# Transposing a as 32-bit pairs of bf16 columns in a two-stage matmul with GELU

## The chip, the cores and the metric

The kernel runs on one core of a Trainium2 chip. The time is device time in microseconds, the median of several runs. The engines are named as the profile names them: PE is TensorE (its weight loads are PEld), DVE is VectorE, ACT is ScalarE, POOL is GpSimd, SP is SyncE, which only issues DMAs here.

## The reference

Inputs are float32: a is 1024 x 1024, b is 1024 x 2048, c is 2048 x 1024.

```python
def reference(a, b, c):
    h = np.matmul(a, b)
    h = 0.5 * h * (1 + np.tanh(np.sqrt(2 / np.pi) * (h + 0.044715 * h ** 3)))
    return np.matmul(h, c).astype(np.float32)
```

## The kernel before

The kernel keeps everything in SBUF as bf16 and writes the program order of every engine by hand (a manual schedule): each engine works its instructions off in the order in which they stand in the code, and waits by semaphores for what the others produce.

TensorE contracts over the partitions, so for h = a b both operands need the contraction index k on the partitions. b has it there as loaded. a does not: it is loaded with its rows on the partitions and must be transposed. The result, aT, has k on the partitions and the rows of a (two halves h = 0, 1 of H = 512) along the free dimension.

The first part of a (halves 0 and 1 of columns 0 to 255, and half 0 of columns 256 to 511) and of b comes by SP's queue as float32 into `sta` and `stb` and is cast to bf16 on VectorE and ScalarE (`cast_a`, `cast_b`). The rest is loaded by POOL's queue with a cast on the way: `abq` for a, `b1` and `b2` for b, `c_sb` for c. These loads stand in one list, and after the eighth each issue waits for the landing of the load eight places ahead of it.

`turn(h, q, i, ab)` is the transposition of 256 columns of a for one half h, in bank i of PSUM. It is a generator: for each n of two blocks of 128 columns it issues four TensorE transposes (128x128 bf16, the piece of a as weights, the identity as the moving operand) and one VectorE copy from PSUM to `aT`; then it yields, and the caller puts matmuls between. Nearly all turns use bank 7.

The stages in order:

1. The first quarter of b's columns, tiles t = 0 to 3 (128 columns each), plainly: `block(h, tiles, ks)` adds the contraction slices ks to the accumulators `ps[h, t]` by `mm1` (one matmul of 128x512, line L114). The eight accumulators (two halves, four tiles) would fill all eight banks, so `ps[1, 3]` is done at the end of the stage and bank 7 serves the turns until then. The k loop follows the arrival of a and b. Turns (0,0), (1,0), (0,1), (1,1), ... stand between the blocks. While the first data is awaited, `stir` issues matmuls on zeros.
2. `seven(zero, ...)`: the second quarter of b's columns, by a scheme of seven products instead of eight (Strassen's, in Winograd's form). Its operands are sums and differences that VectorE makes in float32r: t1 to t4 from the four blocks of aT, s1 to s4 from those of b. Two of the products, P1 and P2, read aT and b directly. The t's are made partly during stage 1 (`zero.t1`, `zero.t2`, `zero.t3`, line L170).
3. `seven(one, ...)`: the other half of b's columns in the same way with the same t's.
4. `seven(two, ...)`: GELU(h) times c, with the seven products again, and the stores.

In stages 2 to 4 the order is P1, P2, P5, P6, P7, and then P4 and P3 (in stage 2) or P3 and P4. All products are issued at line L212. `snap` (L298) copies a PSUM bank to SBUF on ScalarE, `plus` (L303) adds a bank and such a copy on VectorE; the functions `between0` and `between1` place the VectorE work of the operands between the products.

The order around the turns in the loop of stage 1 is, before the change:

```python
    for q in range(1, 3):
        k = 2 * q
        block(0, range(4), (k,))
        tn = turn(1, q, 7, abq[:, q, 1])
        next(tn)
        block(0, range(4), (k + 1,))
        next(tn)
        zero.t1(4, q)
```

Of the kernel before, what the change touches and what calls it, by code (L numbers as in the profile page):

```python
# [9 lines left out]
F32 = mybir.dt.float32  # L10
F32R = mybir.dt.float32r
BF16 = mybir.dt.bfloat16
# [7 lines left out]
def kernel(ctx, tc, a, b, c, out):  # L20
    nc = tc.nc
    M, K = a.shape
    _, N = b.shape
    _, P = c.shape
    H = 512
    KT = K // 128
    NT = N // 128

    av = a.rearrange("(mt p) k -> p mt k", p=128)
    bv = b.rearrange("(kt p) n -> p kt n", p=128)  # L30
    cv = c.rearrange("(nt p) q -> p nt q", p=128)

    ctx.enter_context(tc.manual_schedule())
    consts = ctx.enter_context(tc.tile_pool(name="consts", bufs=1))
# [5 lines left out]
    def slot(tag, shape, dt, name):  # L40
        return big.tile(shape, dt, name=name, tag=tag)

    def bank(i, shape=(128, H), dt=F32, name="ps"):
        return pp.tile(list(shape), dt, name=name, tag=f"bank{i}", padded_shape=None)

    def pieces(tag, bufs, shape, dt, name):
        return small.tile(shape, dt, name=name, tag=tag, bufs=bufs)

    warm = nc.const_aps.tensor(0.0, [128, 256], F32)
    ident = consts.tile([128, 128], BF16, name="ident")  # L50
    make_identity(nc, ident)
    gate = consts.tile([128, 1], F32, name="gate")
    g = consts.tile([128, 1], F32, name="g")

    consts.tile([128, 16], F32, name="room")

    c_sb = keep.tile([128, NT, P], BF16, name="c_sb")
    hT = [keep.tile([128, NT, H], BF16, name=f"hT{h}") for h in range(2)]
    aT = slot("a", [128, 2, KT, H], BF16, "aT")
    b1 = slot("b1", [128, KT, 1024], BF16, "b1")  # L60
    b2 = slot("b2", [128, KT, 1024], BF16, "b2")

# [2 lines left out]
    stb = slot("x0", [128, KT, H], F32, "stb")  # L65
    sta = slot("x1", [128, 2, 2, 4, 256], F32, "sta")
    abq = slot("x3", [128, 4, 2, 4, 256], BF16, "abq")

    def a_part(h, q):
        return av[:, 4 * h:4 * h + 4, ds(q * 256, 256)]  # L70

    def b_part(q):
        return bv[:, 2 * q:2 * q + 2, 0:H]

    nc.sync.dma_start(out=sta[:, 0, 0], in_=a_part(0, 0))  # L75
    nc.sync.dma_start(out=stb[:, 0:2], in_=b_part(0))  # L76
    nc.sync.dma_start(out=sta[:, 1, 0], in_=a_part(1, 0))
    nc.sync.dma_start(out=sta[:, 0, 1], in_=a_part(0, 1))
    nc.sync.dma_start(out=stb[:, 2], in_=bv[:, 2, 0:H])

    nc.gpsimd.tensor_copy(gate, sta[:, 0, 0, 3, 0:1])
    nc.scalar.activation(g, warm[:, 0:1], AF.Gelu_apprx_tanh)
# [2 lines left out]
    def cast_load_a(h, q):  # L85
        nc.gpsimd.dma_start(out=abq[:, q, h], in_=a_part(h, q))

    def cast_load_b(q):
        nc.gpsimd.dma_start(out=b1[:, 2 * q:2 * q + 2, 0:H], in_=b_part(q))

    cast_load_a(1, 1)
    nc.gpsimd.dma_start(out=b1[:, 3, 0:H], in_=bv[:, 3, 0:H])
    for q in range(2, 4):
        cast_load_a(0, q)
        cast_load_b(q)
        cast_load_a(1, q)
    for k in range(0, KT, 4):
        nc.gpsimd.dma_start(out=b1[:, k:k + 4, H:], in_=bv[:, k:k + 4, ds(H, H)])
    for n in range(2):
        for k in range(0, KT, 4):  # L100
            nc.gpsimd.dma_start(out=b2[:, k:k + 4, ts(n, H)],
                                in_=bv[:, k:k + 4, ds(1024 + n * H, H)])
    for t in range(0, NT, 2):
        nc.gpsimd.dma_start(out=c_sb[:, t:t + 2], in_=cv[:, t:t + 2])  # L104

    def copy(eng, dst, src):
        if eng is nc.scalar:
            nc.scalar.activation(dst, src, AF.Copy)
        else:
            nc.vector.tensor_copy(dst, src)  # L110

    def mm1(p, t, h, ks):
        for k in ks:
            nc.tensor.matmul(p, b1[:, k, ts(t, 128)], aT[:, h, k],  # L114
                             start=(k == 0), stop=(k == KT - 1))

    def gelu(t, h, p):
# [2 lines left out]
    ps = {(0, t): bank(t) for t in range(4)}  # L120

    def stir(*widths):

        for w in widths:
            nc.tensor.matmul(ps[0, 3][:, 0:w], warm[:, 0:128], warm[:, 0:w],
                             start=True, stop=True, skip_group_check=True)

    def cast_a(h, q, *engs):

        ab = pieces("ab", 2, [128, 4, 256], BF16, "ab")  # L130
        for i, eng in enumerate(engs):
            w = 256 // len(engs)
            for j, e in enumerate(eng if isinstance(eng, tuple) else (eng,)):
                m = slice(2 * j, 2 * j + 2) if isinstance(eng, tuple) else slice(0, 4)
                copy(e, ab[:, m, ts(i, w)], sta[:, h, q][:, m, ts(i, w)])
        return ab

    def turn(h, q, i, ab):

        banks = i if isinstance(i, tuple) else (i,)  # L140
        pts = [bank(x, (128, 2, H), BF16, "pt") for x in banks]
        for n in range(2):
            pt = pts[n % len(pts)]
            for m in range(4):
                nc.tensor.transpose(pt[:, n, ts(m, 128)], ab[:, m, ts(n, 128)], ident)  # L145
            nc.vector.tensor_copy(aT[:, h, 2 * q + n], pt[:, n])  # L146
            yield

    def cast_b(k, *engs):
        c0 = 0  # L150
        for i, eng in enumerate(engs):
            w = (H - c0) if i == len(engs) - 1 else H // len(engs) // 128 * 128
            copy(eng, b1[:, k, ds(c0, w)], stb[:, k, ds(c0, w)])
            c0 += w

    def block(h, tiles, ks):
        for k in ks:
            for t in tiles:
                mm1(ps[h, t], t, h, (k,))


    class Seven:
        def __init__(self, kt, A, B, s, t, n=4):
            self.kt, self.A, self.B, self.s, self.t, self.n = kt, A, B, s, t, n
# [51 lines left out]
    def pair(i):  # L216
        x = slot(f"x{i}", [128, 2, 4, H], F32R, "x1")
        return x[:, 0], x[:, 1]

    BB = [[aT[:, 0, 0:4], aT[:, 1, 0:4]], [aT[:, 0, 4:8], aT[:, 1, 4:8]]]  # L220

    def quarters(b, c0, w):
        return [[b[:, 0:4, ds(c0, w)], b[:, 4:8, ds(c0, w)]],
                [b[:, 0:4, ds(c0 + w, w)], b[:, 4:8, ds(c0 + w, w)]]]

    zero = Seven(4, quarters(b1, H, 256), BB, [None] * 4, [None] * 4, 2)
    one = Seven(4, quarters(b2, 0, H), BB, [None] * 4, zero.t)

    stir(256, 256, 256, 256, 256)
    tn = turn(0, 0, 4, cast_a(0, 0, nc.vector))  # L230
    next(tn)
    stir(128)
    cast_b(0, nc.vector, nc.vector, nc.scalar)
    next(tn)
    stir(64)
    cast_b(1, nc.scalar)
    ab = cast_a(1, 0, nc.vector, nc.scalar)
    block(0, range(4), (0,))
    block(0, range(2), (1,))
    for _ in turn(1, 0, (7, 6), ab):  # L240
        pass
    block(0, range(2, 4), (1,))
    ab = cast_a(0, 1, (nc.scalar, nc.vector), nc.vector)
    cast_b(2, nc.scalar, nc.scalar)
    for t in range(3):
        ps[1, t] = bank(4 + t)
    zero.t[0], zero.t[1] = pair(2)
    block(1, range(3), (0,))
    tn = turn(0, 1, 7, ab)
    next(tn)  # L250
    block(1, range(3), (1,))
    next(tn)
    zero.t1(4, 0)
    for q in range(1, 3):
        k = 2 * q
        block(0, range(4), (k,))
        tn = turn(1, q, 7, abq[:, q, 1])
        next(tn)
        block(0, range(4), (k + 1,))
        next(tn)  # L260
        zero.t1(4, q)
        block(1, range(3), (k,))
        tn = turn(0, q + 1, 7, abq[:, q + 1, 0])
        next(tn)
        block(1, range(3), (k + 1,))
        next(tn)
    zero.t1(4, 3)
    block(0, range(4), (6, 7))
    zero.t2(2, 0)
    for t in range(4):  # L270
        gelu(t, 0, ps[0, t])
    ps[1, 3] = bank(7)
    mm1(ps[1, 3], 3, 1, range(2))
    tn = turn(1, 3, 0, abq[:, 3, 1])
    next(tn)
    mm1(ps[1, 3], 3, 1, range(2, 5))
    next(tn)
    mm1(ps[1, 3], 3, 1, (5,))
    zero.t[2], x11 = pair(1)
    zero.t[3], x31 = pair(3)  # L280
    zero.plain_t(2, 0)
    zero.t3(2, 0)
    zero.t2(2, 1)
    block(1, range(3), (6, 7))
    mm1(ps[1, 3], 3, 1, range(6, 8))
    for t in range(4):
# [99 lines left out]
    def between0(n):  # L386
        if n == "P1":
            zero.plain_s()
            zero.plain_t(2, 1)
        elif n == "P2":  # L390
            zero.t3(2, 1)
            zero.s3()
            zero.t4(t4, 2)
            one.last_t = t4
            zero.s4(x31[:, :, 256:])
# [19 lines left out]
    zero.s1()  # L415
    zero.s2()
    seven(zero, done0, between0)
    one.s[3] = slot("b1", [128, 2, 4, H], F32R, "x1")[:, 0]
    one.s1()
# [68 lines left out]
```

## Time and profile before

| what | value |
|---|---|
| median of 3 runs | 117.55 us (117.53 to 117.62) |
| span of the profiled execution | 115.7 us |
| its own time beside the span | not recorded apart from the span; the median is 1.85 us above it |
| PE busy | 111.1 us (96%), 542 matmuls and as many weight loads |
| DVE / ACT / POOL busy | 90.0 (78%) / 51.4 (44%) / 17.2 (15%) us |
| granted clock of TensorE | 1.000 |
| DMA | 15.94 MB moved, 138 GB/s mean |

How to read it. The span runs from the first to the last instruction of the profiled execution. In lists of instructions each line has the start and the duration in microseconds, the engine, the line of the code, the operation, out<-in by the program's names, the shapes, how many, and in brackets how long the engine had been idle and what ended that. In groups by line the numbers behind the bar are the busy time in microseconds and the mean duration of one in nanoseconds, and behind the next bar the idle time just before them. Matmuls are pipelined: one lasts some 380 ns in the records while a new one starts every 216 ns, so times on TensorE are taken from start to start.

### The profile page before, as it was taken

How to read it: one execution, taken by the hardware profiler on the slowest of the kernel's cores; microseconds unless marked ns; L12 is line 12 of the kernel's file. 1: busy time of each engine (PE TensorE's matmuls, PEld its weight loads, DVE VectorE, ACT ScalarE, POOL GpSimd, SP SyncE). 2: the span in 40 equal slices, each digit the busy share in tenths (PEclk: the TensorE clock that was granted, in tenths of full speed). 3: DMA queues.
4: the chain of work that ended last, by engine and by line, in shares of the span. 5: the costliest groups of instructions: out<-in, count | busy, mean ns of one | idle time of the engine just before them, and what ended most of it. 6: DMA issues, size and time to landing. Idle time of an engine off the chain costs nothing.

```text
span 115.7 us, 1461 instructions
## 1 busy us (share of the span) xinstructions
PE 111.1 (96%) x542; PEld 77.1 (67%) x542; DVE 90.0 (78%) x107; ACT 51.4 (44%) x86; POOL 17.2 (15%) x29
## 2 busy tenths in 40 slices
PE   7989999999999999999999999999999999999980
PEld 6645555546776447888885444688888888888860
DVE  0347748789999998935699999999999986954770
ACT  5053000999259997166698429500124982000000
POOL 2497755223322000000000000000000000000000
PEclk9999999999999999999999999999999999999999
DMA  2999999999999999998000000060000002014993
GB/s 69 295 381 229 200 199 205 204 208 205 206 211 209 212 213 209 212 210 168 8 0 0 6 0 0 38 235 0 0 0 0 0 4 91 1 73 176 370 363 106
DMA packets 13414, 15.94 MB, mean 138 GB/s; under 512 B 736, under 2 KB 9312, under 8 KB 13408
## 3 DMA queue, kind: packets, MB, share of 16 engines
q0 software_dynamic: 8672, 9.31, 47.6%
q1 hardware_dynamic: 4736, 6.56, 15.8%
q8 instruction: 4, 0.07, 0.3%
q14 instruction: 2, 0.02, 0.0%
HBM read 20.97 MB, written 4.19 MB: 218 GB/s over the span
## 4 chain that ended last, share of the span: by engine, by line
PE 90%; DMA 5%; SPq 1%; DVE 1%; issue 0%
PE ps L212 76%; PE ps L114 11%; DMA sta<-in_a_dram 5%; PE pt L145 3%; SPq L76 0%; DVE ab L110 0%; SPq L75 0%; DVE ot L375 0%
## 5 line engine op out<-in xcount | busy, mean ns | idle before, releaser
L212 PE MATMUL ps<-x,s 128*128 128x512 f32 x128 | 29.6, 391 | 0.0
L212 PEld LDWEIGHTS ps<-x,s 128*128 128x128 f32 x128 | 24.0, 188 | 5.1
L212 PE MATMUL ps<-x,x 128*128 128x512 f32 x96 | 22.9, 394 | 0.0
L212 PEld LDWEIGHTS ps<-x,x 128*128 128x128 f32 x96 | 18.0, 188 | 3.9
L114 PE MATMUL ps<-aT,b 128*128 128x512 bf16 x64 | 16.1, 379 | 0.2 <-DVE b L110 0.2
L298 ACT ACTIVATE v<-ps 128x512 f32<-128x512 f32 x10 | 6.0, 599 | 19.1 <-PE ps L212 19.1
L212 PE MATMUL ps<-c_sb,hT 128*128 128x512 bf16 (+1 forms) x72 | 14.2, 356 | 0.0
L212 PE MATMUL ps<-x 128*128 128x512 f32 x56 | 13.2, 392 | 0.0
L212 PEld LDWEIGHTS ps<-x 128*128 128x128 f32 x56 | 10.2, 188 | 2.6 <-ACT u L298 0.4
L118 ACT ACTIVATE hT<-ps 128x512 bf16<-128x512 f32 x14 | 7.3, 595 | 9.7 <-PE ps L114 9.7
L212 PEld LDWEIGHTS <-hT 128*128 128x128 bf16 x72 | 6.9, 98 | 7.0 <-issue 0.5
L118 ACT ACTIVATE hT<-ot 128x512 bf16<-128x512 f32 x18 | 10.4, 624 | 2.0 <-DVE ot L303 2.0
L212 PE MATMUL ps<-aT,b 128*128 128x512 bf16 x48 | 10.7, 379 | 0.0
L146 DVE COPY aT<-pt 128x512 bf16<-128x512 bf16 x16 | 6.7, 423 | 5.1 <-PE pt L145 5.1
L303 DVE TENSOR_TENSOR ot<-ps,u 128x512 f32<-128x512 f32 x10 | 6.7, 690 | 5.1 <-ACT u L298 5.1
L303 DVE TENSOR_TENSOR ot<-ps,v 128x512 f32<-128x512 f32 x10 | 6.7, 688 | 4.8 <-DMA out_dram<-ot 3.8
L170 DVE TENSOR_TENSOR x<-c_sb 128x1024 fp32r<-128x1024 bf16 x8 | 9.3, 1226 | 0.0
L114 PEld LDWEIGHTS <-b 128*128 128x128 bf16 x64 | 5.7, 98 | 4.5 <-DVE b L110 0.3
L212 PEld LDWEIGHTS <-b 128*128 128x128 bf16 x48 | 4.6, 98 | 5.7 <-issue 0.3
L104 POOL DMA_DIRECT2D c_sb<-in_c_dram x8 | 5.6, 702 | 13.1 <-DMA b<-in_b_dram 12.4
L170 DVE TENSOR_TENSOR x<-b 128x1024 fp32r<-128x1024 bf16 (+1 forms) x4 | 7.0, 1752 | 0.6 <-issue 0.6
L298 ACT ACTIVATE u<-ps 128x512 f32<-128x512 f32 x10 | 5.9, 598 | 3.4 <-PE ps L212 3.2
(44 smaller groups left out, 111.3 us busy)
## 6 DMA issues: line engine op xcount, KB each, us to landing
c_sb<-in_c_dram POOLq DMA_DIRECT2D x8, 512.0 KB, 20.0
out_dram<-ot SPq DMA_DIRECT2D x13, 256.0 KB, 2.1
b<-in_b_dram POOLq DMA_DIRECT2D x6, 512.0 KB, 15.3
sta<-in_a_dram SPq DMA_DIRECT2D x3, 512.0 KB, 6.1
abq<-in_a_dram POOLq DMA_DIRECT2D x5, 256.0 KB, 7.9
out_dram<-ot SPq DMA_DIRECT2D x6, 128.0 KB, 2.0
stb<-in_b_dram SPq DMA_DIRECT2D x1, 512.0 KB, 5.3
b<-in_b_dram POOLq DMA_DIRECT2D x2, 256.0 KB, 8.2
```

Of the source, the lines that this page charges most:

```text
L104: nc.gpsimd.dma_start(out=c_sb[:, t:t + 2], in_=cv[:, t:t + 2])
L114: nc.tensor.matmul(p, b1[:, k, ts(t, 128)], aT[:, h, k], start=(k == 0), stop=(k == KT - 1))
L118: nc.scalar.activation(hT[h][:, t], p, AF.Gelu_apprx_tanh)
L145: nc.tensor.transpose(pt[:, n, ts(m, 128)], ab[:, m, ts(n, 128)], ident)
L146: nc.vector.tensor_copy(aT[:, h, 2 * q + n], pt[:, n])
L170: nc.vector.tensor_tensor(out=dst[:, r], in0=x[:, r], in1=y[:, r], op=op)
L212: nc.tensor.matmul(p[:, ds(c0, w)], l[:, k, ts(j, 128)], r[:, k, ds(c0, w)], start=(start and k == 0), stop=(k == self.kt - 1), skip_group ...
L298: nc.scalar.activation(st, p, AF.Copy)
L303: nc.vector.tensor_tensor(out=ot, in0=p, in1=st, op=ADD)
```

## The change

A bf16 piece of a is taken as 32-bit words, each of two neighbouring columns, and transposed as float32: four transposes of 128x128 words do what eight bf16 ones did. What comes out has on partition p the columns 2p and 2p + 1 of the 256, side by side. The layout of `aT` becomes [128, 2, KT / 2, H, 2], the pair being the last index; one VectorE copy of 512 float32 words per turn takes the place of two of 512 bf16. A contraction slice is therefore no longer 128 neighbouring rows of b, but the even or the odd rows of 256; b is loaded accordingly (`bq`), and the matmuls read every second bf16 of `aT`. The class `Turned` gives stages 2 and 3 the same view of aT.

The turns are now put between single matmuls: `block` takes a generator and issues one transpose ahead of each of its matmuls. The casts of a are split by rows and no longer by columns. The b loads of POOL's queue behind the first are 12 of 256 KB (written) in place of 6 of 512 KB. `zero.t1(4, q)` stands at the end of the loop; `zero.t1(4, 3)`, both halves of `zero.t2` and the first half of `zero.t3` move later.

```diff
-    bv = b.rearrange("(kt p) n -> p kt n", p=128)
+    bq = b.rearrange("(q p r) n -> p q r n", p=128, r=2)
...
-    ident = consts.tile([128, 128], BF16, name="ident")
+    ident = consts.tile([128, 128], F32, name="ident")
...
-    aT = slot("a", [128, 2, KT, H], BF16, "aT")
+    aT = slot("a", [128, 2, KT // 2, H, 2], BF16, "aT")
...
-        return bv[:, 2 * q:2 * q + 2, 0:H]
+        return bq[:, q, :, 0:H]
+
+    def b_load(tile_, q, n0):
+        nc.gpsimd.dma_start(out=tile_[:, 2 * q:2 * q + 2, ds(n0 % 1024, H)], in_=bq[:, q, :, ds(n0, H)])
...
-    for k in range(0, KT, 4):
-        nc.gpsimd.dma_start(out=b1[:, k:k + 4, H:], in_=bv[:, k:k + 4, ds(H, H)])
-    for n in range(2):
-        for k in range(0, KT, 4):
-            nc.gpsimd.dma_start(out=b2[:, k:k + 4, ts(n, H)],
-                                in_=bv[:, k:k + 4, ds(1024 + n * H, H)])
+    for n0, tile_ in ((H, b1), (1024, b2), (1024 + H, b2)):
+        for q in range(4):
+            b_load(tile_, q, n0)
...
-            nc.tensor.matmul(p, b1[:, k, ts(t, 128)], aT[:, h, k],
+            nc.tensor.matmul(p, b1[:, k, ts(t, 128)], aT[:, h, k // 2, :, k % 2],
...
-        banks = i if isinstance(i, tuple) else (i,)
-        pts = [bank(x, (128, 2, H), BF16, "pt") for x in banks]
-        for n in range(2):
-            pt = pts[n % len(pts)]
-            for m in range(4):
-                nc.tensor.transpose(pt[:, n, ts(m, 128)], ab[:, m, ts(n, 128)], ident)
-            nc.vector.tensor_copy(aT[:, h, 2 * q + n], pt[:, n])
+        pt = bank(i, (128, H), F32, "pt")
+        for m in range(4):
+            nc.tensor.transpose(pt[:, ts(m, 128)], ab[:, m].bitcast(F32), ident)
+            if m == 3:
+                nc.vector.tensor_copy(aT[:, h, q].rearrange("p m r -> p (m r)").bitcast(F32), pt)
             yield
...
-    def block(h, tiles, ks):
+    def block(h, tiles, ks, turns=()):
+        turns = iter(turns)
         for k in ks:
             for t in tiles:
+                next(turns, None)
                 mm1(ps[h, t], t, h, (k,))
+        for _ in turns:
+            pass
...
+    class Turned:
+        def __init__(self, h, k0):
+            self.h, self.k0 = h, k0
+
+        def __getitem__(self, at):
+            k = at[1]
+            if isinstance(k, slice):
+                k0, n = self.k0 + k.start, k.stop - k.start
+                q, r = divmod(k0, 2)
+                return aT[:, self.h, q, :, r:r + n].rearrange("p m r -> p r m")
+            q, r = divmod(self.k0 + k, 2)
+            return aT[:, self.h, q, at[2] if len(at) > 2 else slice(0, H), r]
...
     stir(256, 256, 256, 256, 256)
-    tn = turn(0, 0, 4, cast_a(0, 0, nc.vector))
-    next(tn)
-    stir(128)
+    ab = cast_a(0, 0, nc.vector)
+    for n, _ in enumerate(turn(0, 0, 4, ab)):
+        if n == 3:
+            stir(256, 128)
     cast_b(0, nc.vector, nc.vector, nc.scalar)
-    next(tn)
-    stir(64)
     cast_b(1, nc.scalar)
-    ab = cast_a(1, 0, nc.vector, nc.scalar)
+    ab = cast_a(1, 0, (nc.scalar, nc.vector))
     block(0, range(4), (0,))
-    block(0, range(2), (1,))
-    for _ in turn(1, 0, (7, 6), ab):
-        pass
-    block(0, range(2, 4), (1,))
-    ab = cast_a(0, 1, (nc.scalar, nc.vector), nc.vector)
+    block(0, range(4), (1,), turn(1, 0, 7, ab))
+    ab = cast_a(0, 1, (nc.scalar, nc.vector))
     cast_b(2, nc.scalar, nc.scalar)
...
-    block(1, range(3), (0,))
-    tn = turn(0, 1, 7, ab)
-    next(tn)
+    block(1, range(3), (0,), turn(0, 1, 7, ab))
     block(1, range(3), (1,))
-    next(tn)
     zero.t1(4, 0)
     for q in range(1, 3):
         k = 2 * q
-        block(0, range(4), (k,))
-        tn = turn(1, q, 7, abq[:, q, 1])
-        next(tn)
+        block(0, range(4), (k,), turn(1, q, 7, abq[:, q, 1]))
         block(0, range(4), (k + 1,))
-        next(tn)
+        block(1, range(3), (k,), turn(0, q + 1, 7, abq[:, q + 1, 0]))
+        block(1, range(3), (k + 1,))
         zero.t1(4, q)
-        block(1, range(3), (k,))
-        tn = turn(0, q + 1, 7, abq[:, q + 1, 0])
-        next(tn)
-        block(1, range(3), (k + 1,))
-        next(tn)
-    zero.t1(4, 3)
     block(0, range(4), (6, 7))
-    zero.t2(2, 0)
...
-    mm1(ps[1, 3], 3, 1, range(2))
     tn = turn(1, 3, 0, abq[:, 3, 1])
-    next(tn)
-    mm1(ps[1, 3], 3, 1, range(2, 5))
-    next(tn)
-    mm1(ps[1, 3], 3, 1, (5,))
+    for k in range(4):
+        mm1(ps[1, 3], 3, 1, (k,))
+        next(tn)
+    mm1(ps[1, 3], 3, 1, (4, 5))
+    zero.t1(4, 3)
+    zero.t2(2)
     zero.t[2], x11 = pair(1)
     zero.t[3], x31 = pair(3)
     zero.plain_t(2, 0)
-    zero.t3(2, 0)
-    zero.t2(2, 1)
...
         elif n == "P2":
-            zero.t3(2, 1)
+            zero.t3(2)
```

More of the change, by code (lines that the diff above doesn't have):

```diff
@@ L53 @@
     g = consts.tile([128, 1], F32, name="g")
-    consts.tile([128, 16], F32, name="room")
+    consts.tile([128, 80], F32, name="room")
     c_sb = keep.tile([128, NT, P], BF16, name="c_sb")
     hT = [keep.tile([128, NT, H], BF16, name=f"hT{h}") for h in range(2)]
-    aT = slot("a", [128, 2, KT, H], BF16, "aT")
+    aT = slot("a", [128, 2, KT // 2, H, 2], BF16, "aT")
     b1 = slot("b1", [128, KT, 1024], BF16, "b1")
@@ L78 @@
     nc.sync.dma_start(out=sta[:, 0, 1], in_=a_part(0, 1))
-    nc.sync.dma_start(out=stb[:, 2], in_=bv[:, 2, 0:H])
+    nc.sync.dma_start(out=stb[:, 2], in_=bq[:, 1, 0, 0:H])
     nc.gpsimd.tensor_copy(gate, sta[:, 0, 0, 3, 0:1])
@@ L91 @@
     cast_load_a(1, 1)
-    nc.gpsimd.dma_start(out=b1[:, 3, 0:H], in_=bv[:, 3, 0:H])
+    nc.gpsimd.dma_start(out=b1[:, 3, 0:H], in_=bq[:, 1, 1, 0:H])
     for q in range(2, 4):
@@ L218, in pair @@
         return x[:, 0], x[:, 1]
-    BB = [[aT[:, 0, 0:4], aT[:, 1, 0:4]], [aT[:, 0, 4:8], aT[:, 1, 4:8]]]
+    class Turned:
[9 more added lines that the diff above has]
+            return aT[:, self.h, q, at[2] if len(at) > 2 else slice(0, H), r]
+    BB = [[Turned(0, 0), Turned(1, 0)], [Turned(0, 4), Turned(1, 4)]]
     def quarters(b, c0, w):
```

## The prediction

> **What bounds the kernel now.** I read the page first, then the chain of waits that ended last in order of time, then the timeline of the first 38 us, where the changed lines run, and last the groups of instructions by shape for durations.
>
> The page: TensorE is busy for 96% of the span, VectorE for 78%.
>
> ```profile
> span 115.7 us, 1461 instructions
> PE 111.1 (96%) x542; PEld 77.1 (67%) x542; DVE 90.0 (78%) x107; ACT 51.4 (44%) x86; POOL 17.2 (15%) x29
> PE 90%; DMA 5%; SPq 1%; DVE 1%; issue 0%
> PE ps L212 76%; PE ps L114 11%; DMA sta<-in_a_dram 5%; PE pt L145 3%; SPq L76 0%; DVE ab L110 0%; SPq L75 0%; DVE ot L375 0%
> ```
>
> In order of time the chain is a load of a until 7.88, a cast, and from 8.38 to 112.4 TensorE with nothing between its instructions. A stall put in early therefore moves the end, and so does a saved transposition.
>
> ```profile
> 1.78 6.10 DMA sta<-in_a_dram
> 7.90 0.44 DVE ab L110
> 8.38 0.62 PE pt L145 x8
> 24.46 87.96 PE ps L212 x400
> ```
>
> The timeline shows one turn: four transposes, matmuls behind them that do not need them, and the VectorE copy of their result.
>
> ```profile
> 7.90 0.63 ACT L108 ACTIVATE ab<-sta 128x512 bf16<-128x512 f32 x1 [0.43 <-DMA sta<-in_a_dram]
> 7.90 0.43 DVE L110 CAST ab<-sta 128x512 bf16<-128x512 f32 x1 [0.67 <-DMA sta<-in_a_dram]
> 11.93 0.39 PE L145 MATMUL pt<-ident,abq 128*128 128x128 bf16 x4
> 12.15 1.03 PE L114 MATMUL ps<-aT,b 128*128 128x512 bf16 x4
> 12.35 0.42 DVE L146 COPY aT<-pt 128x512 bf16<-128x512 bf16 x1
> ```
>
> Four transposes take 0.22 of TensorE's issue, 0.055 each; a bf16 matmul takes 0.216 (four from 16.15, the next transposes at 17.02). From the last transpose's issue (11.93 + 3 x 0.055 = 12.10) to the start of the copy are 0.26, and TensorE starts 0.06 after a VectorE result (copy 5.58 to 6.00, transposes at 6.06).
>
> These rows give the prices:
>
> ```profile
> L146 DVE COPY aT<-pt 128x512 bf16<-128x512 bf16 x16 | 6.7, 423 | 5.1 <-PE pt L145 5.1
> L434 DVE COPY ot<-ps 128x512 f32<-128x512 f32 x4 | 2.7, 690 | 0.2 <-PE ps L212 0.2
> L125 PE MATMUL ps<-const-float32-0.0 128*128 128x128 f32 x2 | 0.4, 302 | 0.0
> L145 PE MATMUL pt<-ident,abq 128*128 128x128 bf16 x40 | 3.9, 218 | 0.0
> ```
>
> **Part by part.** I follow TensorE from 8.38, where the old chain begins, to the start of L212 at 24.29: 15.91 us. It holds 58 of the 64 L114 matmuls (6 ran before), 58 x 0.216 = 12.53, so transposes and hand-overs took 3.38.
>
> Transposes. 64 become 32; 28 of them stand behind the first four, which run while b is awaited (first matmul at 6.83, when the cast of b is done). A 32-bit transpose is not in the trace. Below is the bf16 one at 0.055, above the f32 matmul of the same 128 columns (two issued from 5.38 to 5.82, so 0.22). I take 0.055, the row of the same operation: 28 x 0.055 = 1.54, a gain of 3.38 - 1.54 = 1.84 before stalls. The f32 weight loads last 188 ns where bf16 ones last 98; each has a 0.216 matmul ahead to hide under, as the f32r weights of L212 do; without that cover it adds about 0.09 x 28 = 2.5.
>
> [...]
>
> The copy. Two of 0.423 become one of 0.69 (L434's shape: 512 f32 out of PSUM). VectorE saves 8 x 0.16, but nothing can use any of the turn before 0.26 + 0.69 + 0.06 = 1.01 after its last transpose. The old pair handed over each half after 0.26 + 0.42 + 0.06 = 0.74, with six or more matmuls before the first use. In the new order:
> - a(1,0): the load lands at 7.86 as before. The first transpose now needs ScalarE's half of the cast (0.63, so 8.53) and not VectorE's (8.33). Only four matmuls go ahead of it in place of six. TensorE starts at 8.62 with 60 matmuls left.
> - Then four pairs of transpose and matmul, the last transpose issuing at 8.62 + 3 x 0.271 = 9.44. The matmuls end at 9.72; block(1,(0,)) needs this copy (9.70 to 10.39): a stall to 10.45, 0.73.
> - a(0,1): its last transpose issues at 10.45 + 3 x 0.271 = 11.27 and only three matmuls stand behind it, 0.055 + 0.65 = 0.70 against 1.01: a stall of 0.31. VectorE's cast for it, behind the copy, ends at 10.82, in time for its third transpose. The same 0.31 comes at a(0,2) and a(0,3): 0.93 for the three. The turns of h = 1 in the loop have five matmuls behind them (1.13) and do not stall.
> - a(1,3): two matmuls behind its last transpose, 0.49 against 1.01: 0.52.
> Stalls 0.73 + 0.93 + 0.52 = 2.18. The stretch ends at 8.62 + 60 x 0.216 + 1.54 + 2.18 = 25.30: 1.01 later than before.
>
> VectorE behind it. zero.t1(4,3) and both halves of t2 move behind the last copy, and the other half of t3 between s2 and s3. The copy ends at 23.53 (last transpose at 22.58). Spacings from the old timeline (0.60 for the short t1, 1.14 for 1024 elements, 1.32 where s2 needs s1): t1 to 24.13, t2 to 26.40, s1 to 27.72, s2, both t3, s3 and two t4 to 34.54, s4 to 35.68, where the first sum of C22 starts. Before, that was 33.94: VectorE is 1.74 later, TensorE only 1.01. s1 and s3 (ready 27.63 and 32.35) are still early for P5 and P7 (28.6 and 32.4); the first half of t4 too, for P4. The products on py need the first sum read out, 35.68 + 0.69 + 0.06 = 36.43, against TensorE at 33.24 + 1.01 + 8 x 0.22 = 36.01: a stall of 0.4, of which I keep 0.34 because P4 itself waits some hundredths for t4's second half or a snap. In the next stage s1 is ready at 40.17 for use at 43.74, so VectorE's lag ends there.
>
> Strided reads. 64 + 48 matmuls now read aT in steps of 4 bytes. Not in the trace; f32r streams, also 4 bytes a column, take 0.2268 (32 from 95.98 in 7.42) against 0.2162 for bf16 (32 from 37.01 in 7.08). Bounds 0 and 112 x 0.0106 = 1.2; I take 0, because those f32r matmuls load f32 weights too, and these do not. [...]
>
> [...]
>
> Loads. The rows of b are regrouped in 2 KB pieces as before. Six L98/L101 issues become twelve: 6 x 0.75 = 4.5 us more on POOL's queue, ahead of the c loads. POOL waits 12.4 us there for b's landing, which covers it. The last part of b1's second half is issued at 14.8 in place of 12.3, when its eighth predecessor lands, but with seven 0.5 MB loads still ahead at 0.41 MB/us (1 MB each 2.55 us, the c loads) it lands at about 25.8 as now, for use at 27.0. Without that cover it lands 2.5 later and costs up to 1.3. Half as many bytes in flight (4 MB) are still 10 us of transfer. The f32 identity is made long before 5.15: nothing.
>
> Sum: +1.01 + 0.34 = +1.35. The profiled execution shows 115.7 of span; the median of 117.55 has 1.85 around it that the change does not touch. 115.7 + 1.35 + 1.85 = 118.9.
>
> **The rivals.**
> A: a 32-bit transpose costs 0.22, as the f32 matmul does. 28 x 0.165 = 4.6 more on TensorE, less little, as every stall starts behind the last transpose: +6.0, 123.5. For it: no row shows a cheaper f32 instruction of this width. [...] 12%.
> B: faster. The copy runs at the 423 ns of the bf16 row, as 512 elements out of PSUM to SBUF also are there. 0.27 leaves each hand-over: 0.73 to 0.46, 0.31 to 0.04 thrice, 0.52 to 0.25, 0.34 to 0.07; 1.62 less, -0.3, 117.3. It decides from a copy of about 0.46. Against it: L434's 690 ns have exactly the new copy's shape. 8%.
> C: reads in steps of two bf16 run at half rate: 112 x 0.216 = 24, 143. Nothing in the trace speaks for it. 4%.
> D: the change leaves the time alone, because VectorE and TensorE recover what is lost: the chain has no wait after 8.4 that could shrink. 3%.
>
> **How the numbers follow.** The forecast has 73%, with 118.0 (a stall of 0.3 less in three places) to 121.4 (strides at 1.2 and uncovered weights at half of 2.5, added to 118.9) as its own range. That leaves out A and C, most of B: about 2 in 10 together with what misses the forecast's ends. No change means within 0.2% of 117.55 (0.24 us), about what a measurement of this kernel can tell. Faster is B, and a little for stalls that overlap: 0.09. Same: D and the edge of B, 0.03. Slower: 0.88.
>
> **What would show it.** Right: the group of 32-bit transposes x32 with about 0.27 from one pair to the next; copies x8 at 690 ns; gaps of TensorE near 8, 9.7, 12, 15.8, 19.5 and 23 us with VectorE's copy of aT as what ended them, 2 to 3 us in all; L212 from about 25.3; the chain through DVE aT. Wrong: L212 starting before 24.3; copies under 0.5; four transposes and four matmuls taking over 1.5 (A); L114 matmuls farther apart than 0.22 where nothing is waited for (C); or a DMA landing of b that ends TensorE's wait near 27.

## The result: 5% slower

The changed kernel takes 1.046 times as long as the kernel before (95% interval 1.044 to 1.048). Its executions lie in two groups, 122.6 to 123.1 us with a mean granted clock of 1.000 and 124.9 to 125.2 us with one of 0.982 to 0.986; the ratio is that of the first group, which I set at 123.05 against 117.52. The forecast was 118.9, with a range to 121.4: the sign and the stalls were right, three prices were too low.

### The profile page after: what moved, and what is told of

The parts are those of the page before. It is cut to its first block, busy times and chain, and to the rows that moved or that the text cites. A ratio compares the mean times of both kernels' runs of the same rounds, so it can differ in the third digit from the quotient of the medians.

```text
span 123.2 us, 1399 instructions
## 1 busy us (share of the span) xinstructions
PE 114.7 (93%) x505; PEld 78.5 (64%) x510; DVE 88.6 (72%) x98; ACT 51.4 (42%) x86; POOL 21.4 (17%) x35
## 4 chain that ended last, share of the span: by engine, by line
PE 83%; DMA 9%; DVE 3%; SPq 2%; issue 1%; ACT 1%
PE ps L214 72%; DMA stb<-in_b_dram 9%; PE ps L114 8%; PE pt L142 3%; DVE aT L144 2%; ACT b L108 1%; SPq L79 1%; SPq L80 0%; SPq L81 0%; SPq L78 0%; DVE ot L374 0%
## 5 line engine op out<-in xcount | busy, mean ns | idle before, releaser
L114 PE MATMUL ps<-aT,b 128*128 128x512 bf16 x62 | 19.5, 413 | 3.1 <-DVE b L110 2.6
L144 DVE COPY aT<-pt 128x512 f32<-128x512 f32 x8 | 5.5, 692 | 12.6 <-PE pt L142 12.6
L114 PEld LDWEIGHTS <-b 128*128 128x128 bf16 x64 | 6.5, 102 | 9.7 <-DVE b L110 2.8
L214 PE MATMUL ps<-aT,b 128*128 128x512 bf16 x47 | 11.1, 387 | 0.1
L76 POOL DMA_DIRECT2D b<-in_b_dram x12 | 8.4, 704 | 9.1 <-DMA abq<-in_a_dram 5.5
L214 PEld LDWEIGHTS <-b 128*128 128x128 bf16 x48 | 4.5, 96 | 6.3 <-issue 0.3
```

Source lines behind the costliest of these rows:

```text
L76: nc.gpsimd.dma_start(out=tile_[:, 2 * q:2 * q + 2, ds(n0 % 1024, H)], in_=bq[:, q, :, ds(n0, H)])
L114: nc.tensor.matmul(p, b1[:, k, ts(t, 128)], aT[:, h, k // 2, :, k % 2], start=(k == 0), stop=(k == KT - 1))
L144: nc.vector.tensor_copy(aT[:, h, q].rearrange("p m r -> p (m r)").bitcast(F32), pt)
L214: nc.tensor.matmul(p[:, ds(c0, w)], l[:, k, ts(j, 128)], r[:, k, ds(c0, w)], start=(start and k == 0), stop=(k == self.kt - 1), skip_group ...
```

## The profile after

The page of the changed kernel. In its profiled execution the granted clock falls to half for 3.4 us.

```profile
span 123.2 us, 1399 instructions
...
PE 114.7 (93%) x505; PEld 78.5 (64%) x510; DVE 88.6 (72%) x98; ACT 51.4 (42%) x86; POOL 21.4 (17%) x35
...
PE 83%; DMA 9%; DVE 3%; SPq 2%; issue 1%; ACT 1%
PE ps L214 72%; DMA stb<-in_b_dram 9%; PE ps L114 8%; PE pt L142 3%; DVE aT L144 2%; ACT b L108 1%; SPq L79 1%; SPq L80 0%; SPq L81 0%; SPq L78 0%; DVE ot L374 0%
```

Two entries are new in the chain that ended last: VectorE's copy of aT with 2%, which the forecast named, and a load of b into `stb` with 9%, which it did not. In order of time that second entry is the last of SP's five loads, the third slice of `stb`:

```profile
3.09 10.62 DMA stb<-in_b_dram
```

What TensorE waits for first, however, is the first load into `stb`, which stands ahead of it on the same queue. The timeline shows it; the first fence is the kernel before, the second the changed one. The columns are start, duration, engine, line, operation, and in brackets the idle time before.

```profile
6.54 0.94 ACT L108 ACTIVATE b<-stb 128x256 bf16<-128x256 f32 x2 [4.30 <-DMA stb<-in_b_dram]
```

```profile
3.09 1.97 SPq L82 DMA_DIRECT2D stb<-in_b_dram  x1
...
9.32 0.94 ACT L108 ACTIVATE b<-stb 128x256 bf16<-128x256 f32 x2 [7.09 <-DMA stb<-in_b_dram]
...
9.88 1.89 PE L114 MATMUL ps<-aT,b 128*128 128x512 bf16 x4 [2.58 <-DVE b L110]
...
10.68 0.63 ACT L108 ACTIVATE ab<-sta 128x512 bf16<-128x512 f32 x1 [0.42 <-DMA sta<-in_a_dram]
```

The first slices of b are there at 9.32 where the kernel before had them at 6.54, and the next piece of a (10.68 in place of 7.90), behind it on the same queue, is as late. TensorE stands still for 2.58 us. The DMA issues by line give the same in microseconds from issue to landing; before, these three were 6.1, 5.3 and 7.1.

```profile
sta<-in_a_dram SPq DMA_DIRECT2D x3, 512.0 KB, 8.8
...
stb<-in_b_dram SPq DMA_DIRECT2D x1, 512.0 KB, 8.1
stb<-in_b_dram SPq DMA_DIRECT2D x1, 256.0 KB, 10.6
```

The windows by microsecond show the clock (the figure ahead of the last two): it falls to 0.50 at the end of the idle stretch and is back in the window from 13 to 14 us (0.85), 3.4 us in all. The four matmuls from 9.88 start 0.43 apart.

```profile
9.00:10.00 1.00, 0.12 (x1) 0.12 (x2) 0.57 (x2) 0.68 (x2) 1.00 (x3) 0.94 1.20 318
10.00:11.00 1.00, 1.00 (x3) 0.34 (x3) 0.32 (x1) 0.57 (x2) 1.00 (x2) 0.50 1.37 226
```

At full clock the stream of the first stage looks like this, a turn of h = 1:

```profile
17.37 0.27 PE L142 MATMUL pt<-ident,abq 128*128 128x128 f32 x1
...
17.48 0.39 PE L114 MATMUL ps<-aT,b 128*128 128x512 bf16 x1
...
17.71 0.27 PE L142 MATMUL pt<-ident,abq 128*128 128x128 f32 x1
...
17.81 1.29 PE L114 MATMUL ps<-aT,b 128*128 128x512 bf16 x4
18.01 0.69 DVE L144 COPY aT<-pt 128x512 f32<-128x512 f32 x1 [0.83 <-PE pt L142]
```

From a 32-bit transpose to the matmul behind it are 0.11 (17.37 to 17.48), where the forecast had 0.055, and from a matmul to the next start 0.23, where bf16 had 0.216. The copy lasts 0.69, as L434 had promised.

## The experiments

Theory at the start: beside the forecast's terms, the way in which SP's loads read b costs the late start. Rival: something else in the changed program delays them. Each ratio is to the kernel before, measured beside the run on the same chip.

**1. The changed kernel with the old rows in SP's loads.**

```diff
-    nc.sync.dma_start(out=stb[:, 0:2], in_=b_part(0))
+    nc.sync.dma_start(out=stb[:, 0:2], in_=bv[:, 0:2, 0:H])
...
-    nc.sync.dma_start(out=stb[:, 2], in_=bq[:, 1, 0, 0:H])
+    nc.sync.dma_start(out=stb[:, 2], in_=bv[:, 2, 0:H])
```

> The changed kernel, but SP's two loads of b into stb take the rows as before (128 neighbouring rows for each contraction slice), so the first contraction slices pair wrong rows of b and the output differs; instructions and bytes are the same. Theory L: reading b in pairs of rows is what made SP's loads land late (stb at 9.3 us in place of 6.5), and the loads behind them on that queue. Then stb lands at about 6.5, the first matmul starts at about 6.8, and the time falls by 2.5 to 3 us to about 120.3. Rival W: the late landing comes from something else in the changed program (issue order, the POOL loads); then 123 stays. The forecast's own price for the rest (118.9) plus 28 transposes at 0.11 in place of 0.055 us (1.5) also gives 120.4.

Measured: 121.19 (ratio 1.030, 1.028 to 1.032), with a granted clock of 0.997 to 1.000 in all four executions. stb is there at 6.44:

```profile
6.44 0.94 ACT L109 ACTIVATE b<-stb 128x256 bf16<-128x256 f32 x2 [4.20 <-DMA stb<-in_b_dram]
```

So the rows that SP's loads read are worth 1.9 us (123.05 to 121.19), and 3.6 of the loss remain, 0.8 more than the expectation had put there. This run, at full clock, is the one against which the forecast's terms can be checked; its timeline around a stall of h = 0:

```profile
11.73 0.27 PE L143 MATMUL pt<-ident,ab 128*128 128x128 f32 x1
...
11.84 0.84 PE L115 MATMUL ps<-aT,b 128*128 128x512 bf16 x3
12.04 0.69 DVE L145 COPY aT<-pt 128x512 f32<-128x512 f32 x1 [0.93 <-PE pt L143]
...
12.78 0.14 PEld L143 LDWEIGHTS pt<-ident,abq 128*128 128x128 f32 x1 [0.62 <-DVE aT L145]
12.78 0.33 PE L143 MATMUL pt<-ident,abq 128*128 128x128 f32 x1
```

The last transpose issues at 11.73, the next TensorE instruction that needs its copy starts at 12.78: 1.05, against the 1.01 of the forecast. Three matmuls fill 11.84 to 12.52; the rest is the stall.

**2. The kernel before with pair rows in SP's two loads of b.**

```diff
-    nc.sync.dma_start(out=stb[:, 0:2], in_=b_part(0))
+    nc.sync.dma_start(out=stb[:, 0:2], in_=bq[:, 0, :, 0:H])
...
-    nc.sync.dma_start(out=stb[:, 2], in_=bv[:, 2, 0:H])
+    nc.sync.dma_start(out=stb[:, 2], in_=bq[:, 1, 0, 0:H])
```

> The kernel before, but SP's two loads of b into stb take rows in pairs as the changed kernel does; the output differs for that reason. Theory L: stb lands near 9.3 us and the time rises by 2 to 3 us to about 120. Rival W: 117.5, no change.

Measured: 121.68 (ratio 1.036, 1.032 to 1.039). Two changed loads alone cost 4.1 us, the lowered clock included that follows the idle stretch in the profiled execution (0.60 on the average from 10 to 14 us); in all four executions the granted clock was 0.972 to 0.985 over the whole span.

```profile
9.41 0.94 ACT L109 ACTIVATE b<-stb 128x256 bf16<-128x256 f32 x2 [7.18 <-DMA stb<-in_b_dram]
```

The rival falls: 9.41, close to the 9.32 of the changed kernel, with nothing else changed.

**3 and 4. What about the pairs is slow: two ways of splitting the first load.**

```diff
+    for r in range(2):
+        nc.sync.dma_start(out=stb[:, r], in_=bq[:, 0, r, 0:H])
```

> The changed kernel with the first load into stb as two loads, one for the even and one for the odd rows: same rows to the same partitions, but no two neighbouring rows in one DMA. Theory L1 (the pairs merge to one run of 256 rows, which is shared out unevenly among the DMA engines): stb lands near 6.8, time near 120.5. Theory L2 (the rows that the engines read at the same time lie badly in memory): stb stays near 9 us, time 122.5 to 123.5.

```diff
+    for i in (0, 64):
+        nc.sync.dma_start(out=stb[i:i + 64, 0:2], in_=bq[i:i + 64, 0, :, 0:H])
```

> The changed kernel with the first load into stb as two loads of 64 partitions each, the pairs kept. Theory L1: the uneven share stays, stb near 9 us, time near 123. Theory L2: the engines then read 64 KB apart in place of 128 KB, as they did before the change; stb lands near 7, time near 120.7.

Measured: by row 122.17 (ratio 1.038, 1.035 to 1.042), one of five executions at 124.81 with the clock down (0.986); by halves 122.44 and 122.62 (ratio 1.042, 1.039 to 1.044), two more at 124.99 and 126.21 with the clock down (0.983 and 0.973). The arrivals, first by halves, then by row (even rows, odd rows):

```profile
9.25 0.94 ACT L109 ACTIVATE b<-stb 128x256 bf16<-128x256 f32 x2 [7.02 <-DMA stb<-in_b_dram]
```

```profile
6.01 0.42 ACT L109 ACTIVATE b<-stb 128x256 bf16<-128x256 f32 x1 [3.78 <-DMA stb<-in_b_dram]
...
8.65 0.63 ACT L109 ACTIVATE b<-stb 128x512 bf16<-128x512 f32 x1 [2.22 <-DMA stb<-in_b_dram]
```

By halves stb lands at 9.25, so the spacing of the engines' shares (L2) is not it. By row the even rows are there by 6.01, the odd ones at 8.65: better, not cured, which L1 alone did not foresee.

**5 and 6. The kernel before, first load with rows 3p, 3p + 1 and with rows 4p, 4p + 1.**

```diff
+    br = b[0:384, :].rearrange("(p r) n -> p r n", r=3)
+    nc.sync.dma_start(out=stb[:, 0:2], in_=br[:, 0:2, 0:H])
```

> The kernel before, but its first load into stb takes rows 3p and 3p + 1 of b for partition p (not the rows that the products need, so the output differs); each of the 16 shares of 8 partitions then begins 24 rows (192 KB) after the one before it, in place of 64 KB in the kernel before and 128 KB in the changed one. Theory L2 (spacings of 128 KB and larger powers of two make engines collide in memory): 192 KB is no such spacing, stb lands near 6.2 and the time stays at 117.5 to 118.2. Theory L3 (any neighbouring pair of rows on one partition is slow): near 121.5, as with the pairs alone.

> The same with rows 4p and 4p + 1, shares 32 rows (256 KB) apart. L2: as slow as the pairs alone (121.7) or slower. L3: near 121.5 too. If both this and the one with 3p stay near 117.5, it is the run of 256 consecutive rows and neither theory holds.

Measured: 117.69 (ratio 1.001, 0.999 to 1.004) and 118.01 (1.004, 1.002 to 1.005). stb with 3p, then with 4p:

```profile
6.35 0.94 ACT L109 ACTIVATE b<-stb 128x256 bf16<-128x256 f32 x2 [4.12 <-DMA stb<-in_b_dram]
```

```profile
5.71 0.94 ACT L109 ACTIVATE b<-stb 128x256 bf16<-128x256 f32 x2 [3.47 <-DMA stb<-in_b_dram]
```

In these two runs neighbouring rows on one partition are not slow (6.35 and 5.71, against 6.54 in the kernel before), nor is a larger power of two between the shares (256 KB in place of 64, 5.71). What is left is that 256 rows follow each other without a gap. In the built program the source of that one load is written as 256 rows by 512, while its destination is 128 partitions by 2 by 512; the fast ones of this load have 128 by 2 by 512 on both sides.

**7. The price of reading every second bf16.** The kernel of experiment 1, with neighbouring reads by the matmuls and the same dependencies:

```diff
-            nc.tensor.matmul(p, b1[:, k, ts(t, 128)], aT[:, h, k // 2, :, k % 2],
+            nc.tensor.matmul(p, b1[:, k, ts(t, 128)], aT[:, h, k // 2].rearrange("p m r -> p (m r)")[:, ds((k % 2) * H, H)],
```

and the same in `Turned` for the matmuls.

> The changed kernel with the old rows of b in SP's loads, and besides the 112 matmuls that read aT read 512 neighbouring bf16 of it in place of every second one; the values that they meet are wrong and only the pattern of the reads differs. Theory S (the upper bound of the forecast's strided term is what it costs): 112 x 0.0105 = 1.2 us less than the 121.2 of the kernel with the old rows, 120.0; the matmuls of line L115's kind start 0.216 apart in place of 0.2265. Rival: the spacing of 0.2265 comes from something else (the transposes between them), and the time stays at 121.2.

Measured: 120.42 (ratio 1.024, 1.021 to 1.026), 0.8 below experiment 1. The groups by line, first of experiment 1, then of this one (busy time, mean ns):

```profile
L115 PE MATMUL ps<-aT,b 128*128 128x512 bf16 x64 | 18.2, 388 | 1.0 <-DVE b L111 0.6 <-DVE aT L145 0.3
L215 PE MATMUL ps<-aT,b 128*128 128x512 bf16 x48 | 11.2, 388 | 0.0
```

```profile
L115 PE MATMUL ps<-aT,b 128*128 128x512 bf16 x64 | 17.6, 379 | 0.7 <-DVE aT L145 0.4 <-DVE b L111 0.3
L215 PE MATMUL ps<-aT,b 128*128 128x512 bf16 x48 | 10.7, 379 | 0.0
```

The mean falls by 9 ns, and from start to start, where no transpose or wait stands between, the matmuls go from 0.226 to 0.216. S holds: 112 x 0.010 = 1.1. Of that 0.8 arrives: with shorter matmuls less time covers the copies, and the five waits for them grow from 2.1 to 2.2 in all; the remaining 0.2 I did not trace.

**8. TensorE kept busy while b is awaited.**

```diff
-            stir(256, 128)
+            stir(256, 128, *[256] * 5)
```

> The changed kernel with five more matmuls on zeros (2.1 us) behind the first four transposes, while b is awaited. Theory G: TensorE's idle time of 2.6 us ahead of the first matmul is what lets the granted clock fall to half for some 4 us in part of the executions; with it filled, the runs near 125 us vanish and all lie at 122.5 to 123.2, the granted clock 1.0 throughout. Rival: the clock falls for another reason and runs near 125 remain.

Measured: 123.02, 124.61, 124.87 and 125.37. The long times stay, and theory G fails as it was put. Only the longest had the clock down (0.986): in its profile TensorE still waits from 8.6 to 10.0 and around 11.3, and the clock falls at 12 (0.51 from 12 to 14 us) in place of 10. The two of 124.61 and 124.87 ran at a granted clock of 1.000, so here something other than the clock made them late; neither was profiled, and what it was stays open. That idle time as such costs the clock is therefore neither shown nor refuted; what experiments 1 and 11 show is that with b in time the clock stays at 0.997 or more, with no time near 125, in four executions each.

**9 and 10. Which of the two loads.** The kernel before with only the first, and with only the third slice's load changed (the diffs of experiment 2, one each).

> The kernel before, but only SP's first load into stb takes the rows of b in pairs (2p and 2p + 1); the third slice keeps the old rows. In the program the source of that load becomes one run of 256 rows where all the others have 128 partitions by 2 rows. Theory M (that form of the load is slow): stb lands near 9.3 us as with both loads changed, and the time rises by 2.5 to 4 us, 120 to 121.7. Theory T (it is the third slice's load, at every second row, that holds the queue up): 117.5 to 118.

> The kernel before, but only SP's last load, the third slice of stb, takes every second row of b. Theory M: 117.5, its landing at 9.6 to 10 us. Theory T: its landing goes to 12 us or later, and the time rises by 1 to 3 us, since the matmuls of that slice follow at about 11 us.

Measured: first only 121.43 (ratio 1.030, 1.025 to 1.036), again with a lowered granted clock in all four executions (0.972 to 0.983; in the profiled one 0.50 from 10 to 12 us); third only 117.99 (1.002, 0.999 to 1.006), not to be told from no change, its landing at 10.69 against 9.98 before. The first load of the first-only run:

```profile
9.43 0.94 ACT L109 ACTIVATE b<-stb 128x256 bf16<-128x256 f32 x2 [7.20 <-DMA stb<-in_b_dram]
```

It is the first load, the one that became 256 consecutive rows.

**11. The changed kernel, complete, with the pair stored in reverse.** The same 256 rows to the same partitions, but with a step of -1 the source can't be one run.

```diff
-    nc.sync.dma_start(out=stb[:, 0:2], in_=b_part(0))
+    nc.sync.dma_start(out=stb[:, 0:2], in_=bq[:, 0, ::-1, 0:H])
...
-            copy(eng, b1[:, k, ds(c0, w)], stb[:, k, ds(c0, w)])
+            copy(eng, b1[:, k, ds(c0, w)], stb[:, (1, 0, 2)[k], ds(c0, w)])
```

> The changed kernel, complete, with the two rows of each pair put into stb in reverse order, so that the source can't be one run of 256 rows; the same rows are read by the same partitions, and the casts pick the slices accordingly. Theory M: stb lands near 6.5 to 7, the first matmul starts at about 7.4, and the time falls to about 121.2 to 121.8. If it is the rows themselves (which engines read what at one time), stb stays near 9 us and the time at 122.6 to 123.1, with runs near 125.

Measured: 121.68 (ratio 1.034, 1.031 to 1.038), 121.45 to 121.85 with none near 125.

```profile
7.14 0.94 ACT L108 ACTIVATE b<-stb 128x256 bf16<-128x256 f32 x2 [4.91 <-DMA stb<-in_b_dram]
```

and among the DMA issues:

```profile
stb<-in_b_dram SPq DMA_DIRECT2D x1, 512.0 KB, 5.9
```

Theory M holds: the same rows go to the same partitions, and the load takes 5.9 us in place of 8.1, so it is not which rows are read but how the load is written. What the transfer does differently is not shown by itself: that the one run is the reason is argued from the built program and from experiments 5, 6 and 11, and the reversal also changes the order of the two rows. The trace adds that a few parts of the load are late and not all: its 16 completions in the changed kernel lie between 5.4 and 9.3 us with the middle one at 6.4, in the kernel before between 6.0 and 6.5; in this run the last is in by 7.14. The change recovers 1.4 of the 1.9. The load is still 0.7 slower than in experiment 1 (5.9 against 5.2), and the turn of a(1,0) starts at 9.19 against 8.48, enough for the last 0.5; why, is open, and so is the late odd row of experiment 3, a load that is no single run. This is the better form of the changed kernel, and still slower than the kernel before.

**12. The copy cut short.** The kernel of experiment 7; the copy still waits for the last transpose, but moves 64 words of 512.

```diff
-                nc.vector.tensor_copy(aT[:, h, q].rearrange("p m r -> p (m r)").bitcast(F32), pt)
+                nc.vector.tensor_copy(aT[:, h, q].rearrange("p m r -> p (m r)").bitcast(F32)[:, 448:512], pt[:, 448:512])
```

> The kernel with the old rows of b and neighbouring reads (120.4), with VectorE's copy of a turn cut to its last 64 words of 512, so that it still waits for the last transpose but takes about 0.2 us in place of 0.69; most of aT then keeps zeros that are written at the start. The forecast's stall terms depend on that length: 0.48 less in the wait at a(1,0) and in that at a(1,3), and the three of about 0.3 vanish, 1.8 together: 118.7. If the waits are for something else (bank 7, the casts), the time stays above 120.

Measured: 118.96 (ratio 1.012, 1.009 to 1.015), 1.5 below experiment 7 with 1.8 expected. What is missing is a new wait that the shorter copies lay open:

```profile
15.50 0.23 DVE L146 COPY aT<-pt 128x64 f32<-128x64 f32 x1 [1.94 <-PE pt L144]
...
16.30 0.30 PE L144 MATMUL pt<-ident,abq 128*128 128x128 f32 x1 [0.19 <-DMA abq<-in_a_dram]
```

TensorE is ready for the next piece of a at 15.95, before it has landed, and loses 0.35; in the chain that ended last TensorE's part now begins behind this load, at 16.17. The run settles a rival too. In experiment 1 the profile puts the longest of these waits down to a cast of b on ScalarE (first fence). With the short copy the same transpose starts at 10.29, while that cast runs from 9.94 to 10.66 (second fence), so TensorE does not wait for the cast:

```profile
10.70 0.30 PE L143 MATMUL pt<-ident,ab 128*128 128x128 f32 x1 [0.65 <-ACT b L109]
```

```profile
9.94 0.72 ACT L110 ACTIVATE b<-stb 128x256 bf16<-128x256 f32 x2
...
10.29 0.30 PE L144 MATMUL pt<-ident,ab 128*128 128x128 f32 x1 [0.19 <-DVE aT L146]
```

The stalls were the copy's, as the forecast had it, and the loads are next.

## Why the prediction was wrong, by its own steps

Experiment 1 has every term but the load. In its first stage TensorE's starts add up as follows, beside the forecast:

```
                                             forecast      measured
start of the turn at a(1,0)                    8.62          8.48
60 matmuls                             60 x 0.216 = 12.96   60 x 0.226 = 13.56
28 transposes behind the first four    28 x 0.055 =  1.54   28 x 0.108 =  3.02
stalls                                         2.18          2.28
L212/L215 starts                              25.30         27.42 (sum 27.34)
```

- **Stalls behind the one copy: right.** Forecast 0.73, three times 0.31 and 0.52; measured 0.81, three times 0.27 and 0.49, and 0.17 more where a weight load waits with its transpose. Experiment 12 shows that the copy's length makes them.
- **The 32-bit transpose: mis-sized, 1.5 us.** I took the bf16 row's 0.055; it takes 0.108, twice that. The other end, 0.22, was misread: it came from the ends of two records (5.38 to 5.82), and one f32 matmul of the program shows as two records (seven matmuls of `stir`, 14 records). At full clock the second of two such records of 128 columns starts 0.11 after the first (0.38 less the 0.27 that the last one lasts, in the changed kernel):

```profile
6.92 0.38 PE L125 MATMUL ps<-const-float32-0.0 128*128 128x128 f32 x2
```

So the transpose costs what one such record does, half of a whole f32 matmul; the price was that of the f32 row, read from start to start, and not that of the bf16 row. Where the granted clock was 0.50, a transpose and the matmul behind it go 0.20 apart in place of 0.11 (12.21 to 12.41 in the changed kernel).
- **Strided reads: mis-sized, 0.6 us in the first stage and 0.5 in the next two.** I argued that the f32r stream's 0.2268 came from its f32 weights and took 0. The upper bound was the price: 0.226. Experiment 7 shows 10 ns a matmul (0.226 against 0.216).
- **VectorE behind the last copy, 0.34: not there.** The forecast had VectorE 1.74 late and TensorE 1.01, a distance of 0.73. In experiment 1 VectorE's first sum is 3.67 late and TensorE's stream of P7 3.26 (34.68 against 31.42), a distance of 0.41. The slack that the kernel before had at this point (0.36: the third product starts at 31.42 + 16 x 0.227 = 35.05, the first sum is read out by 33.94 + 0.69 + 0.06 = 34.69) covers nearly all of it. First the kernel before, then experiment 1:

```profile
33.94 1.28 DVE L303 TENSOR_TENSOR ot<-ps,u 128x512 f32<-128x512 f32 x2
```

```profile
37.61 1.29 DVE L303 TENSOR_TENSOR ot<-ps,u 128x512 f32<-128x512 f32 x2
```

`L215`'s stream of P7, P4 and P3 has no new gap (24 matmuls from 34.68 to 40.31 against 31.42 to 37.01 before: 5.63 and 5.59).
- **The loads: the step that failed.** "The rows of b are regrouped in 2 KB pieces as before" counted bytes and pieces, and then priced POOL's queue alone, where, as forecast, no wait of TensorE came of it. SP's first load was put at nothing without a look, though all of the start hangs on it: it lands after 8.1 us in place of 5.3. It costs 1.9 us at full clock and 3.8 in the profiled execution, where the clock falls (124.95 against 121.19).

The sum: 1.35 + 1.5 (transposes) + 1.1 (strides) - 0.3 (VectorE) = 3.6, which is experiment 1 (121.19 - 117.62 = 3.57), and 1.9 for the load make 5.5, the measured 123.05 - 117.52. Of the gain hoped for, 64 transposes for 32, hardly anything was there to be had: 28 x 0.108 and 60 x 0.010 are 3.6 on TensorE against the 3.4 that transposes and hand-overs took before. Rival A at half its price and the top of the stride bound were both true at once; the range had added the stride to half of another cost, but no load.

## What to carry to other kernels

A layout change is priced at every reader and at every load that feeds it: here the form of the first load on the critical queue was worth 1.9 us with the bytes unchanged (512 KB, 8.1 us to land against 5.2), and a source that merges into one long run while its destination does not should be looked at in the built program. Where two rows of the trace bracket an operation that it doesn't show, the near row is a hope: read both from start to start, and let the sum decide whether the change survives the far one. Halving the number of copies gained nothing on TensorE here: one of 0.69 us took the place of two of 0.42, and where the matmuls behind it filled less than the 1.05 from the last transpose to its first use, TensorE waited, 2.1 in all in experiment 1.

## What the runs showed of the hardware

- A 32-bit transpose of 128x128 words holds TensorE for 0.108 us, the bf16 one for 0.055; at a granted clock of 0.50 the 32-bit one took 0.20. An f32 matmul of 128 columns shows as two records 0.11 apart.
- A bf16 matmul whose moving operand steps by 4 bytes starts every 0.226 us, with neighbouring elements every 0.216.
- An HBM load issued from SP whose source was one run of 256 rows of 2 KB took 8.1 us to land; with the same rows written as 128 by 2 in reverse order 5.9. The load of rows 3p and 3p + 1 was in by 6.35 us, the one of 256 rows in a run by 9.32. The loads behind it on the queue were late by as much or more (the next piece of a by 2.8 us, the third slice of b by 3.75).
- At a 32-bit transpose that waited for VectorE's copy its weight load started with it and not ahead (both at 12.78 in experiment 1; 8.65 and 8.88 at one that did not wait), and the matmul behind it came 0.06 later: 12.95, 0.17 behind in place of 0.11.
- The granted clock went to 0.50 for 3.4 us after TensorE had stood still for 2.6 us, in the profiled execution of the changed kernel; its executions with the lowered clock (0.982 to 0.986) took 1.9 us longer (124.95 against 123.05).
